# The mixer begins on half of K while the other half's modulation still loads

## The chip, the cores and the metric

One core of one Trainium2 chip runs the whole program. The metric is the device time of one execution in microseconds. Five engines work beside one another, each in the order of its own queue: TensorE (PE in the rows), VectorE (DVE), ScalarE (ACT), GpSimd (POOL) and SyncE (SP), which here only issues transfers. A transfer is issued by an engine's queue (SPq, ACTq) and carried out by 16 DMA engines.

## The reference

A first block (a mixer of forgetting attention and a gated linear recurrence, then a product-key expert layer, "peer"), and a second block (an S5 state-space layer, then an attention layer with compressed, selected and windowed keys), on 256 tokens of width 2048, all in float32. What matters for the change is the beginning of the first block:

```python
sc = jax.nn.silu(c)
mod = sc @ w_ada[l] + b_ada[l]                    # (1, 2048) @ (2048, 12288)
sh1, sc1, ga1, sh2, sc2, ga2 = jnp.split(mod, N_ADA, axis=-1)
h = _rmsnorm(x, g_mix[l]) * (1.0 + sc1[:, None, :]) + sh1[:, None, :]
...
proj = h @ w_in                                   # q, k, v, f, lx, ly
```

`sh1` and `sc1` must be known before `h`, and `h` before every projection. `w_ada` falls into twelve blocks of 1024 columns: 0 and 1 are `sh1`, 2 and 3 `sc1`, 4 and 5 `ga1`, 6 to 9 `sh2` and `sc2`, 10 and 11 `ga2`. Channels 0 to 1023 of `h`, the first half of K of the projections, need blocks 0 and 2 alone; channels 1024 to 2047 need 1 and 3. The second block has 16 such blocks more (`mod_w0`, `kv_mod_w`, `mod_w1`).

## The kernel before

Activations lie transposed, as sixteen tiles of 128 channels by 256 tokens. A product in near-float32 precision is made of three fp32r products: weights and activations are each split into a high and a low part. A half of a weight strip (128 x 1024, 0.52 MB, eight k) is loaded by SyncE into `raw` (four buffers), cast on ScalarE to `wh` and subtracted on VectorE or GpSimd to `wl` (three buffers each; `half`, L335). For each k, `step_b` (L353) multiplies `wh` with both parts of the activation, which lie side by side, in one product of 512 columns, and `wl` with the high part in one of 256; `ev` (L409) adds the two results. For the values, `lin_a` (L389) has the activations as the stationary side and makes three products of 512 columns.

The modulation is a product of one vector with a wide matrix (`gemv`, L284). In the form `big` it is summed on TensorE: chunks of 2 MB come into the four `xs` buffers, and four small products per k (`columns`, L291) add up in `pg`. Otherwise chunks of 0.52 MB come into `graw` (two buffers) from SyncE's queue (L299), and VectorE multiplies and adds them in `gacc` (L310, L312) if a buffer for it is open, with TensorE only for the sum over partitions. This form is a generator in `self.bg`: every weight strip's `tick` (L167) advances it by `self.rate` steps; at the end of a block it yields `PAUSE` up to three times, each of which ends the steps of that tick; `need` runs what is left, and `pace` (L185) sets a rate from it.

`start` (L515) loads blocks 0, 2, 1, 3 in the form `big` (16 loads of 2 MB), forms the two normed halves of `h` with `normed` (L468, its first operation is L473) and, between them, the set-up of the S5 layer (`s5_setup`, L1033): arithmetic on VectorE, then sixteen steps of `turn` (its first operation is L1126), drained before the mixer. `self.gate` puts the first weight loads behind the 13th of the 16 in SyncE's queue. Then come q (five strips at a time on their first halves), k, f, v, lx, ly and `w_out`; meanwhile the background runs at 1.5 steps a tick, at 3 during lx and ly, and through `w_out` at a rate that `pace` sets so that block 9 (`ffn`) is done. The order on each queue is laid down when the program is built, by priority in the order of the code and by when operands and buffers are free in a model of the run.

Of the kernel before, what the change touches and what calls it, by code (L numbers as in the profile page):

```python
# [9 lines left out]
F = mybir.dt.float32  # L10
# [3 lines left out]
AF = mybir.ActivationFunctionType  # L14
OP = mybir.AluOpType
# [15 lines left out]
TR = 0.45  # L31
TB = 1
NS1 = 5
NET = 4
MP = 1
# [7 lines left out]
NN = 3  # L43
NQ = 5
GA = 12
S2 = 2.5
# [31 lines left out]
COLS = {}  # L78
PAUSE = 2


# [75 lines left out]
class K:  # L157
    def __init__(self, tc, A, dbg=None):
        self.tc, self.nc, self.A = tc, tc.nc, A
        self.dbg = dbg or {}  # L160
        self.full = True
        self.nw, self.pool_share, self.srate = 0, 0, 1
        self.bg, self.side, self.par, self.loads = [], [], [], []
        self.loaded, self.gate, self.gp, self.hold, self.mid = None, None, None, None, False
        self.rate, self.owed, self.sowed, self.towed, self.slow = 1.5, 0.0, 0.0, 0.0, None

# [115 lines left out]


    def gemv(self, w, blocks, which, bias, out, big=False):  # L284
        nc = self.nc
        for b in blocks:
# [9 lines left out]
            for k in range(KD):  # L296
                if not big:
                    raw = self.sb.tile([128, 1024], F, name="graw", tag="graw", bufs=2)
                    nc.sync.dma_start(raw, w[128 * k:128 * k + 128, c0])  # L299
                else:  # L300
                    if k % 4 == 0:
                        rt = self.xs(F).rearrange("p a b t -> p (a b t)").rearrange("p (a c) -> p a c", a=4)
                        self.loads.append(
                            nc.sync.dma_start(rt, w[128 * k:128 * k + 512, c0].rearrange("(a p) c -> p a c", a=4)))
                    raw = rt[:, k % 4]
                ck = self.cact[:, 16 * which + k:16 * which + k + 1]
                if acc is None:
                    columns(ck.to_broadcast([128, 32]), raw, k == 0, k == KD - 1)
                elif k == 0:
                    nc.vector.tensor_scalar(acc, raw, ck, None, op0=OP.mult)  # L310
                else:
                    nc.vector.scalar_tensor_tensor(acc, raw, ck, acc, op0=OP.mult, op1=OP.add)  # L312
                if k < KD - 1:
                    yield True
# [199 lines left out]

    def start(self, x):  # L515
        nc, A, cp = self.nc, self.A, self.cp
        mod = self.mod = cp.tile([128, 96], F, name="mod")
        first = self.gemv(A["w_ada"], (0, 2, 1, 3), 0, self.col("b_ada", 0, 96), mod, big=True)
        for _ in range(8):
            next(first)  # L520
        with self.after(self.loads[0]):
            nc.sync.dma_start(x, A["xT"])
        next(first)
        acc = None
        for k in range(KD):
            acc = self.ssq(acc, x[:, k], k == KD - 1)
        r = self.rstd(acc, D)
        g = cp.tile([128, KD], F, name="gm", tag="gm", bufs=2)
        self.hs = []
        for h in range(2):  # L530
            blocks = 0
            while blocks < 2:
                blocks += not next(first)
                if h == 1 and blocks == TB:
                    next(turn, None)
            c = slice(8 * h, 8 * h + 8)
            nc.vector.scalar_tensor_tensor(g[:, c], mod[:, 16 + 8 * h:24 + 8 * h], 1.0, self.col("g_mix", 8 * h, 8),
                                           op0=OP.add, op1=OP.mult)
            self.hs.append(self.xs())
            self.normed([x[:, k] for k in range(KD)[c]], r, g[:, c], mod[:, c], [self.hs[h]])  # L540
            if h == 0:
                turn, store = self.s5_setup()
                self.side.append(store)
        self.drain([turn])
        self.gate = self.loads[GA]

    def mixer(self, x):
        with self.phase("ph_set") as self.ph:
            self.start(x)
        with self.phase("ph_mixer") as self.ph:  # L550
            self._mixer(x)

    def _mixer(self, x):
        nc, A, sb, cp = self.nc, self.A, self.sb, self.cp
        mod, hs = self.mod, self.hs
        bias = self.col("b_ada", 0, 96)
        self.use_pool(self.ph if GP[0] else None)
# [10 lines left out]
        qk = self.xs(F)  # L568
        for h, p in enumerate(self.lin_bs(A["w_q"], hs, NQ)):
            self.ev(p, qk[:, h, 0], 128 ** -0.5)  # L570
            self.gate = None
        for h in range(8):
            self.ev(self.lin_b(A["w_k"][h], hs), qk[:, h, 1])

        pf = self.lin_b(A["w_f"][0], hs)
        fl = self.s1()[:8]
        f2 = self.s1()[:8]
        nc.scalar.activation(f2, pf[:8, 0], AF.Identity, bias=self.col("b_f")[:8])
        nc.vector.tensor_add(fl, pf[:8, 1], f2)
        ft = self.ph.tile([128, 16], F, name="ft")  # L580
# [27 lines left out]
        self.par.append(decay())  # L608

        va = self.xs(F)  # L610
        vn = va.rearrange("p a b t -> p (a b t)")[:, :2048].rearrange("p (t c) -> p t c", t=2)
        at = va.rearrange("p a b t -> p (a b t)")[:, 2048:].rearrange("p (h t) -> p h t", h=8)
        for c in range(2):
            pp = self.lin_a(A["w_v"][c], hs)
            for t in range(2):
                nc.scalar.copy(vn[:, t, 512 * c:512 * c + 512], pp[t])
        lw = self.t8()
        lwf = lw.rearrange("p a b -> p (a b)")
        nc.sync.dma_start(lwf, A["lru_w"])
        aa, sq, ix = self.t8(), self.t8(), self.t8()  # L620
        ms = [self.xs(), self.xs()]
# [55 lines left out]
        for n in range(8):  # L677
            lx = self.ph.tile([128, T + 3], F, name="lx", tag="lx", bufs=2)
            nc.gpsimd.memset(lx[:, :3], 0.0)
            self.ev(self.lin_b(A["w_lx"][n], hs), lx[:, 3:])  # L680
            g = gates(n, lx)
# [350 lines left out]

    def s5_setup(self):  # L1033
        nc, A, sb, cp = self.nc, self.A, self.sb, self.cp
# [58 lines left out]
        def cmul(o, xr, xi, y):  # L1093

            wr, wi, yr, yi = wide(xr), wide(xi), y[:, :, 0], y[:, :, 1]
            t = self.sb.tile([128, 1024], F, name="graw", tag="graw", bufs=2)
            t = t.rearrange("p (k j c) -> p k j c", k=16, j=4)
# [7 lines left out]
            yield True  # L1105

        b, bb, c = big(), big(), big()
        flat = lambda m: m.rearrange("p k i j c -> p (k i j c)")
# [505 lines left out]
```

## Time and profile before

| | us |
|---|---|
| median of 3 runs | 3625.65 (3624.92 to 3626.92) |
| the profiled execution | 3617.7 |
| its span | 3616.0 |

| engine | busy us | share of the span |
|---|---|---|
| TensorE | 3294.4 | 91% |
| VectorE | 2652.5 | 73% |
| ScalarE | 1700.7 | 47% |
| GpSimd | 1066.7 | 29% |

The stages, as the trace places them: the start until 121 us, q, k, f and v until 292, lx and ly until about 440, `w_out` from 430 to 585, the router and the experts from 605 to 2390, S5 until about 2700, the second attention until the end. A table of busy time by stretch shows which engine is full in which stage; a wait names the engine that came last. Matmuls overlap their weight loads, and their ends are modelled, so the distance between two starts is read for the cost of one, not its duration.

### The profile page before, as it was taken

To read this page: it belongs to the slowest core of one execution; us is meant where nothing else is said; L and a number is where in the kernel's file an instruction comes from. 1 tells how busy PE (TensorE), PEld (TensorE's weight loads), DVE (VectorE), ACT (ScalarE), POOL (GpSimd) and SP (SyncE) were. 2 spreads that over 40 slices of the span, in tenths; PEclk is the share of its full clock that TensorE was granted. 3 is DMA by queue.
4 is the path that set the end of the run, shared out by engine and by line. 5 is a ranking of instruction groups with operands and counts; after the bars stand their busy time and mean duration, and the time that the engine had idled before them with its cause. 6 is when DMAs were issued, how large, how long until landed. Compare 5 with 4: busy or idle time off the path is not lost.

```text
span 3616.0 us, 50453 instructions
## 1 busy us (share of the span) xinstructions
PE 3294.4 (91%) x18446; PEld 2726.2 (75%) x18446; DVE 2652.5 (73%) x4072; ACT 1700.7 (47%) x2789; POOL 1066.7 (29%) x892
## 2 busy tenths in 40 slices
PE   4988778999999999999999989988989989999998
PEld 1676666878777777777777777767878878888886
DVE  4778987997657778887777767779886565666665
ACT  1534544455544444554444433354545544555553
POOL 1123345666522121211211233035452320122223
PEclk7999989999999999999999999989999999999999
DMA  9697676567779888888888878744435556444444
GB/s 398 235 301 252 203 234 228 163 223 262 243 250 314 300 281 291 293 285 279 293 286 278 293 268 269 267 158 139 147 127 186 186 167 198 160 155 149 159 143 144
DMA packets 260409, 832.47 MB, mean 230 GB/s; under 512 B 25792, under 2 KB 66880, under 8 KB 257472
## 3 DMA queue, kind: packets, MB, share of 16 engines
q1 hardware_dynamic: 258096, 829.11, 68.0%
q8 instruction: 145, 2.38, 0.3%
q14 instruction: 104, 0.85, 0.1%
q10 hardware_dynamic: 2064, 0.13, 0.0%
HBM read 797.56 MB, written 31.59 MB: 229 GB/s over the span
## 4 chain that ended last, share of the span: by engine, by line
PE 46%; DVE 14%; DMA 13%; issue 6%; POOL 3%; ACT 1%; SPq 0%; DVEq 0%; POOLq 0%; ACTq 0%
PE p L357 22%; PE p L358 11%; DVE wl L346 5%; DMA graw<-mod_w 5%; DMA graw<-kv_mod_w 3%; PE pm L929 2%; PE pm L928 2%; PE pm L930 2%; DVE gacc L312 2%; DMA s5d<-tb 2%; DMA raw<-peer_u 1%; DVE xs L1286 1%; PE pm L882 1%; ACT wh L342 1%; POOL xs L913 1%
## 5 line engine op out<-in xcount | busy, mean ns | idle before, releaser
L357 PE MATMUL p<-xs,wh 128*128 128x512 f32 x5600 | 2038.6, 406 | 43.5 <-DVE xs L476 19.9
L358 PE MATMUL p<-xs,wl 128*128 128x256 f32 x5600 | 1595.6, 285 | 47.6 <-DVE wl L346 40.4
L342 ACT CAST wh<-raw 128x1024 fp32r<-128x1024 f32 x996 | 1038.4, 1048 | 1124.6 <-PE p L357 408.9
L346 DVE TENSOR_TENSOR wl<-raw,wh 128x1024 fp32r<-128x1024 f32 x904 | 1151.4, 1281 | 511.0 <-ACT wh L342 501.4
L357 PEld LDWEIGHTS p<-xs,wh 128*128 128x128 f32 x5600 | 1069.5, 191 | 321.1 <-issue 39.0
L358 PEld LDWEIGHTS p<-xs,wl 128*128 128x128 f32 x5600 | 1078.4, 193 | 74.5 <-DVE wl L346 58.3
L312 DVE SCALAR_TENSOR_TENSOR gacc<-graw,cact,gacc 128x1024 f32<-128x1024 f32 x315 | 448.8, 1425 | 154.5 <-DMA graw<-mod_w 90.2
L929 PE MATMUL pm<-wl,xs 128*128 128x512 f32 x1024 | 411.7, 402 | 25.3 <-DVE wl L346 24.7
L928 PE MATMUL pm<-wh,xs 128*128 128x512 f32 x1024 | 409.4, 400 | 24.2 <-DVE vacc L937 18.8
L930 PE MATMUL pm<-wh,xs 128*128 128x512 f32 x1024 | 405.8, 396 | 0.0
L346 POOL TENSOR_TENSOR wl<-raw,wh 128x1024 fp32r<-128x1024 f32 x92 | 231.8, 2524 | 305.1 <-ACT wh L342 273.1
L909 POOL TENSOR_TENSOR t<-t,t 128x256 f32<-128x256 f32 x128 | 138.3, 1114 | 589.3 <-DMA t<-wd 589.3
L929 PEld LDWEIGHTS pm<-wl,xs 128*128 128x128 f32 x1024 | 196.2, 192 | 85.1 <-DVE wl L346 45.6
L913 POOL TENSOR_TENSOR xs<-t,xs 128x256 fp32r<-128x256 f32 x128 | 150.6, 1207 | 355.0 <-ACT xs L911 354.9
L928 PEld LDWEIGHTS pm<-wh,xs 128*128 128x128 f32 x1024 | 196.0, 191 | 74.9 <-DVE vacc L937 22.1
L930 PEld LDWEIGHTS pm<-wh,xs 128*128 128x128 f32 x1024 | 196.3, 192 | 39.7
L439 POOL TENSOR_TENSOR ssq<-ssq,s 128x256 f32<-128x256 f32 x96 | 105.4, 1107 | 237.7 <-ACT s L435 235.8
L898 ACT ACTIVATE t<-et 128x256 f32<-128x256 f32 x128 | 53.8, 420 | 209.4 <-DVE et L414 209.2
L413 ACT COPY et<-p 128x256 f32<-128x256 f32 x281 | 102.2, 364 | 31.2 <-PE p L358 31.1
L1528 POOL TENSOR_SCALAR t<-t,st 128x128 f32<-128x128 f32 (+1 forms) x64 | 77.6, 1224 | 128.0 <-DVE st L1526 128.0
L872 DVE TENSOR_SCALAR xs<-iof,eT,eT 128x128 f32<-128x128 f32 x192 | 82.2, 487 | 37.9 <-PE pm L882 37.9
L414 DVE TENSOR_TENSOR et<-p,et 128x256 f32<-128x256 f32 x224 | 93.1, 416 | 10.3 <-ACT et L413 10.3
(392 smaller groups left out, 3126.3 us busy)
## 6 DMA issues: line engine op xcount, KB each, us to landing
raw<-peer_u SPq DMA_DIRECT2D x256, 512.0 KB, 5.3
raw<-peer_v SPq DMA_DIRECT2D x256, 512.0 KB, 5.6
graw<-mod_w SPq DMA_DIRECT2D x192, 512.0 KB, 5.6
graw<-w_ada SPq DMA_DIRECT2D x128, 512.0 KB, 4.8
raw<-nsa_z SPq DMA_DIRECT2D x96, 512.0 KB, 3.7
xs<-w_ada SPq DMA_DIRECT2D x16, 2048.0 KB, 13.1
graw<-kv_mod_w SPq DMA_DIRECT2D x64, 512.0 KB, 5.7
raw<-w_out SPq DMA_DIRECT2D x32, 512.0 KB, 5.1
```

Of the source, the lines that this page charges most:

```text
L312: nc.vector.scalar_tensor_tensor(acc, raw, ck, acc, op0=OP.mult, op1=OP.add)
L342: nc.scalar.copy(h, s)
L346: (nc.gpsimd if on_pool else nc.vector).tensor_sub(l, s, h.bitcast(F))
L357: self.nc.tensor.matmul(p, h[:, sl], x, start=k == 0, stop=False, skip_group_check=True)
L358: self.nc.tensor.matmul(p[:, 1], l[:, sl], x[:, 0], start=False, stop=k == KD - 1, skip_group_check=True)
L413: nc.scalar.copy(t, p[:, 0])
L439: nc.gpsimd.tensor_add(acc[0], acc[0], sq)
L909: nc.gpsimd.tensor_mul(gc, gc, wv[:, c])
L913: nc.gpsimd.tensor_sub(ap[:, c - 2, 1], gs[:, c - 2], ap[:, c - 2, 0].bitcast(F))
L928: nc.tensor.matmul(pp[t], ah, h[:, sl], start=c == 0, stop=False, skip_group_check=True)
L929: nc.tensor.matmul(pp[t], ah, l[:, sl], start=False, stop=False, skip_group_check=True)
L930: nc.tensor.matmul(pp[t], ap[:, c, 1, 128 * t:128 * t + 128], h[:, sl], start=False, stop=c == 7, skip_group_check=True)
```

## The change

`start` loads only blocks 0 and 2 in the form `big` (8 loads of 2 MB). The square sums and the whole S5 arithmetic are traced before the modulation's end, two turns go beside each of the last four steps, and the remaining eight become a generator that each tick advances by one. Weight loads are put behind the 6th of the 8 loads (`GA` 5).

Then the mixer runs in two passes. The first works on the first half of K alone: the eight halves of `w_q`, of `w_k`, the one of `w_f`, both column halves of `w_v`, and four strips of `w_lx` (`NL`). It uses `sum_b`, which makes three products of 256 columns per k into one result, and stores the partial sums (`qk`, `f2`, `vn`, `ix`). Meanwhile blocks 1 and 3 are a background entry `mix`, at 1.85 steps a tick (`RA`); as no `gacc` is open then, its chunks are summed by TensorE. The other blocks wait (`hold` is `ga1`). When `mix` is done the second normed half is made. The second pass does the second halves of the same strips and adds the partial sums; there the background goes on at 0.75 steps a tick (`R1 / 2`), with a tick for every half strip of q, k and f and every strip of v. The rest of lx, ly and `w_out` are as before.

All small modulation chunks, those of the later stages too, are issued from ScalarE's queue by `fetch_chunk`, up to two ahead (`DEEP`), into three `graw` buffers instead of two. The ring `et` has three buffers instead of four. Cut to its core:

```diff
-NET = 4
+NET = 3
-NQ = 5
-GA = 12
+GA = 5
+NL = 4
+RA = 1.85
+DEEP = 2
+    def fetch_chunk(self):
+        if self.chunks:
+            src = self.chunks.pop(0)
+            raw = self.sb.tile([128, 1024], F, name="graw", tag="graw", bufs=3)
+            self.nc.scalar.dma_start(raw, src)
+            self.ahead.append(raw)
...
                 if not big:
-                    raw = self.sb.tile([128, 1024], F, name="graw", tag="graw", bufs=2)
-                    nc.sync.dma_start(raw, w[128 * k:128 * k + 128, c0])
+                    while not self.ahead:
+                        self.fetch_chunk()
+                    raw = self.ahead.pop(0)
...
+                if not big:
+                    while len(self.ahead) < DEEP and self.chunks:
+                        self.fetch_chunk()
...
-        first = self.gemv(A["w_ada"], (0, 2, 1, 3), 0, self.col("b_ada", 0, 96), mod, big=True)
+        first = self.gemv(A["w_ada"], (0, 2), 0, self.col("b_ada", 0, 96), mod, big=True)
...
+        turn, store = self.s5_setup(norm)
+        for n, _ in enumerate(first):
+            if n >= 20:
+                next(turn)
+                next(turn)
+        self.side += [turn, store]
+        self.gate = self.loads[GA]
...
+    def sum_b(self, src, i):
+        self.tick()
+        h, l = self.half(src, i)
+        self.gate = None
+        p = self.p2()[:, 0]
+        for k in range(8):
+            x = self.hs[i][:, k]
+            sl = slice(128 * k, 128 * k + 128)
+            self.nc.tensor.matmul(p, h[:, sl], x[:, 0], start=k == 0, stop=False, skip_group_check=True)
+            self.nc.tensor.matmul(p, h[:, sl], x[:, 1], start=False, stop=False, skip_group_check=True)
+            self.nc.tensor.matmul(p, l[:, sl], x[:, 0], start=False, stop=k == 7, skip_group_check=True)
+        return p
...
-        for n, b in (("ga1", (4, 5)), ("ffn", range(6, 10)), ("ga2", (10, 11))):
+        for n, b in (("mix", (1, 3)), ("ga1", (4, 5)), ("ffn", range(6, 10)), ("ga2", (10, 11))):
...
-        self.rate, self.hold = R1, "ga2"
+        self.rate, self.hold = RA, "ga1"
+        self.pool_share = MP2
+        self.first_half(x, r, 0)
...
+        for h in range(8):
+            nc.scalar.activation(qk[:, h, 0], self.sum_b(A["w_q"][h], 0), AF.Copy, scale=128 ** -0.5)
+        for h in range(8):
+            nc.scalar.copy(qk[:, h, 1], self.sum_b(A["w_k"][h], 0))
+        nc.scalar.activation(f2, self.sum_b(A["w_f"][0], 0)[:8], AF.Identity, bias=self.col("b_f")[:8])
+        values(0)
+        for n in range(NL):
+            nc.scalar.copy(ix[:, n], self.sum_b(A["w_lx"][n], 0))
+            late()
+        self.need("mix")
+        late()
+        self.use_pool(self.ph if GP[0] else None)
+        self.rate, self.hold = R1 / 2, "ga2"
         self.pool_share = MP
...
-            self.ev(self.lin_b(A["w_k"][h], hs), qk[:, h, 1])
+            nc.vector.tensor_add(qk[:, h, 1], self.sum_b(A["w_k"][h], 1), qk[:, h, 1])
```

`values(i)` is `lin_a` for one half of K, `late` makes the second normed half as soon as `mix` is done, and `first_half` holds the lines that formed one normed half in `start`.

## Rows read from the trace of the kernel before

**Rows 1.** The page: span, then busy time, share and instructions of an engine.
```profile
span 3616.0 us, 50453 instructions
...
PE 3294.4 (91%) x18446; PEld 2726.2 (75%) x18446; DVE 2652.5 (73%) x4072; ACT 1700.7 (47%) x2789; POOL 1066.7 (29%) x892
```

**Rows 2.** Busy time by stage: us, engines (instructions), PEclk, DMA share, GB/s.
```profile
core 0: us, PE busy (x) PEld busy (x) DVE busy (x) ACT busy (x) POOL busy (x), PEclk, DMA share, GB/s
0.00:57.00 57.00, 24.21 (x264) 10.56 (x264) 9.63 (x32) 9.56 (x23) 11.04 (x21) 0.84 0.99 396
57.00:121.00 64.00, 44.02 (x387) 24.85 (x387) 48.03 (x168) 30.40 (x92) 0.00 (x0) 0.77 0.76 294
121.00:290.00 169.00, 149.87 (x753) 122.77 (x753) 130.05 (x172) 65.66 (x84) 30.94 (x15) 0.96 0.87 287
290.00:430.00 140.00, 112.49 (x612) 95.39 (x612) 129.02 (x199) 75.38 (x165) 56.44 (x36) 0.94 0.67 219
430.00:505.00 75.00, 47.67 (x229) 39.31 (x228) 64.83 (x105) 26.24 (x49) 18.71 (x10) 0.77 0.65 211
505.00:605.00 100.00, 85.08 (x479) 67.54 (x478) 76.17 (x94) 44.10 (x71) 57.51 (x38) 0.95 0.75 256
```

**Rows 3.** Timeline of the start: start us, us, engine, line, operation, tiles, count.
```profile
54.42 1.28 DVE L473 SCALAR_TENSOR_TENSOR s<-x,gm,rstd 128x256 f32<-128x256 f32 x3
...
83.41 0.69 ACT L1126 ACTIVATE pad<-t,rmask 128x128 f32<-128x128 f32 x2 [12.00 <-DVE t L1104]
...
120.79 0.50 PE L357 MATMUL p<-xs,wh 128*128 128x512 f32 x1
```

**Rows 4.** Timeline of TensorE: products of w_q, and the last two of w_v.
```profile
123.45 0.40 PE L357 MATMUL p<-xs,wh 128*128 128x512 f32 x1
...
123.68 0.28 PE L358 MATMUL p<-xs,wl 128*128 128x256 f32 x1
...
123.80 0.40 PE L357 MATMUL p<-xs,wh 128*128 128x512 f32 x1
...
291.65 0.39 PE L403 MATMUL pm<-wl,xs 128*128 128x512 f32 x1
291.88 0.39 PE L405 MATMUL pm<-wh,xs 128*128 128x512 f32 x1
```

**Rows 5.** Modulation loads issued from 95 to 292, and from 292 to 605.
```profile
graw<-w_ada SPq DMA_DIRECT2D x36, 512.0 KB, 5.5
...
graw<-w_ada SPq DMA_DIRECT2D x67, 512.0 KB, 4.4
```

**Rows 6.** Timeline: twelve of the modulation's small products on TensorE.
```profile
102.60 1.06 PE L293 MATMUL pg<-xs,cact 128*32 128x256 f32 x12
```

**Rows 7.** The page's groups: busy, mean ns of one, then idle before.
```profile
L312 DVE SCALAR_TENSOR_TENSOR gacc<-graw,cact,gacc 128x1024 f32<-128x1024 f32 x315 | 448.8, 1425 | 154.5 <-DMA graw<-mod_w 90.2
```

**Rows 8.** Timeline of VectorE at the end of w_out: the modulation's last steps.
```profile
571.82 1.75 DVE L312 SCALAR_TENSOR_TENSOR gacc<-graw,cact,gacc 128x1024 f32<-128x1024 f32 x1
585.67 0.17 DVE L331 TENSOR_TENSOR mod<-pm,cols 128x8 f32<-128x8 f32 x1 [3.63 <-PE pm L329]
```

**Rows 9.** Waits from 120 to 560: us in total, times, longest.
```profile
DVE gacc L312 <- DMA graw<-w_ada: 21.7, 16, 2.8
```

**Rows 10.** Waits from 1030 to 2200, beside the experts.
```profile
ACT wh L342 <- PE pm L930: 227.5, 114, 9.3
DVE wl L346 <- ACT wh L342: 121.1, 93, 6.7
DVE gacc L312 <- DMA graw<-mod_w: 71.5, 54, 3.8
DVE gacc L312 <- DMA graw<-kv_mod_w: 40.2, 37, 2.8
PE p L358 <- DVE wl L346: 25.2, 25, 2.9
PE pm L929 <- DVE wl L346: 22.6, 31, 2.0
```

**Rows 11.** SyncE's waits from 1030 to 2200, and ScalarE's one load (timeline).
```profile
SPq L339 <- DVE wl L346: 447.4, 233, 7.5
SPq L299 <- DVE gacc L312: 109.7, 83, 3.7
...
120.44 0.39 ACTq L1147 DMA_DIRECT2D s5d<-direct  x1
```

More of the change, by code (lines that the diff above doesn't have):

```diff
@@ L281, in consts, with _gemv @@
         nc.vector.tensor_scalar(self.cact, self.cact, 0.5, None, op0=OP.mult)
-    def gemv(self, w, blocks, which, bias, out, big=False):
+    def fetch_chunk(self):
[4 more added lines that the diff above has]
+            self.ahead.append(raw)
+    def gemv(self, w, blocks, which, bias, out, big=False):
+        nc = self.nc
+        if not big:
+            self.chunks += [w[128 * k:128 * k + 128, 1024 * b:1024 * b + 1024] for b in blocks for k in range(KD)]
+        return self._gemv(w, blocks, which, bias, out, big)
+    def _gemv(self, w, blocks, which, bias, out, big):
         nc = self.nc
@@ L522, in start @@
             nc.sync.dma_start(x, A["xT"])
[L523 to L528, printed above, removed]
-        self.hs = []
[L530 to L543, printed above, removed]
@@ L544, in start, with norm @@
-        self.drain([turn])
-        self.gate = self.loads[GA]
+        rs = []
+        def norm():
+            acc = None
+            for k in range(KD):
+                acc = self.ssq(acc, x[:, k], k == KD - 1)
+            rs.append(self.rstd(acc, D))
+        turn, store = self.s5_setup(norm)
[5 more added lines that the diff above has]
+        self.gate = self.loads[GA]
+        self.g0 = cp.tile([128, KD], F, name="gm", tag="gm", bufs=2)
@@ new lines, in start, with first_half @@
+        self.hs = []
+        return rs[0]
+    def first_half(self, x, r, h):
+        c = slice(8 * h, 8 * h + 8)
+        g, mod = self.g0, self.mod
+        self.nc.vector.scalar_tensor_tensor(g[:, c], mod[:, 16 + 8 * h:24 + 8 * h], 1.0,
+                                            self.col("g_mix", 8 * h, 8), op0=OP.add, op1=OP.mult)
+        self.hs.append(self.xs())
+        self.normed([x[:, k] for k in range(KD)[c]], r, g[:, c], mod[:, c], [self.hs[h]])
+    def sum_b(self, src, i):
[10 more added lines that the diff above has]
+        return p
@@ new lines, in _mixer, with late, values @@
+        fl = self.ph.tile([8, T], F, name="fl")
+        ix = self.t8()
+        def late():
+            if len(hs) == 1 and self.bg[0][0] != "mix":
+                self.first_half(x, r, 1)
+        def values(i):
+            for c in range(2):
+                pp = [self.pm(), self.pm()]
+                for a in range(2):
+                    w = self.wload(A["w_v"][c][2 * i + a])
+                    for kk in range(4):
+                        k = 4 * a + kk
+                        h, l = w[kk // 2]
+                        sl = slice(512 * (kk % 2), 512 * (kk % 2) + 512)
+                        for t in range(2):
+                            xh, xl = (hs[i][:, k, j, 128 * t:128 * t + 128] for j in range(2))
+                            nc.tensor.matmul(pp[t], xh, h[:, sl], start=k == 0, stop=False, skip_group_check=True)
+                            nc.tensor.matmul(pp[t], xh, l[:, sl], start=False, stop=False, skip_group_check=True)
+                            nc.tensor.matmul(pp[t], xl, h[:, sl], start=False, stop=k == 7, skip_group_check=True)
+                    if i == 0:
+                        late()
+                        self.tick()
+                for t in range(2):
+                    o = vn[:, t, 512 * c:512 * c + 512]
+                    if i == 0:
+                        nc.scalar.copy(o, pp[t])
+                    else:
+                        nc.vector.tensor_add(o, o, pp[t])
@@ L579, in _mixer @@
-        nc.vector.tensor_add(fl, pf[:8, 1], f2)
+            nc.vector.scalar_tensor_tensor(qk[:, h, 0], self.sum_b(A["w_q"][h], 1), 128 ** -0.5, qk[:, h, 0],
+                                           op0=OP.mult, op1=OP.add)
+        for h in range(8):
+            nc.vector.tensor_add(qk[:, h, 1], self.sum_b(A["w_k"][h], 1), qk[:, h, 1])
+        nc.vector.tensor_add(fl, self.sum_b(A["w_f"][0], 1)[:8], f2)
         ft = self.ph.tile([128, 16], F, name="ft")
@@ L608, in _mixer @@
         self.par.append(decay())
[L610 to L616, printed above, removed]
+        values(1)
         lw = self.t8()
@@ L679, in _mixer @@
             nc.gpsimd.memset(lx[:, :3], 0.0)
[L680 removed]
+            if n < NL:
+                nc.vector.tensor_add(lx[:, 3:], self.sum_b(A["w_lx"][n], 1), ix[:, n])
+            else:
+                self.ev(self.lin_b(A["w_lx"][n], hs), lx[:, 3:])
             g = gates(n, lx)
@@ L1105, in cmul @@
             yield True
+        before()
         b, bb, c = big(), big(), big()
```

27 lines of the change are left out of this document (12 added, 15 removed).

## The prediction

> **What bounds the kernel now.** I read the page first, then the busy time stage by stage, then the order of work around the first product, then the waits. The profiled execution took 3617.7 us, of which the span is 3616.0 [rows 1]; the median of the runs, 3625.65, is 8 us above it. I sum against 3617.7 and add the 8 us at the end. 0.2% of the time, about what a measurement of this kernel can tell from no change, is 7 us.
>
> TensorE carries the kernel in most places, but not at the start and not evenly. The busy time by stage [rows 2] is read by column. Until 57 us DMA is full (0.99 of its engines) and TensorE runs only the modulation's vector products. From 57 to 121 us DMA falls to 0.76 and TensorE still has no projection: the first normed half begins at 54.4, yet the first w_q product stands at 120.8 [rows 3], since blocks 1 and 3 of w_ada (another 16.8 MB) are loaded ahead of any weight, and then come the sixteen padded turns of the S5 set-up, from 83.4. From 121 to 290 TensorE (150 of 169 us) and DMA (0.87) are both near full. From 290 to 505 it is VectorE: 194 of 215 us busy. In w_out, 505 to 605, TensorE has 85 and VectorE 76 of 100. So an earlier start gains time only if the later stages don't fill with what it pushed back.
>
> **What the change does, part by part.**
>
> *Start.* The first stage now loads 8 chunks of 2 MB, not 16, so the normed first half comes where it comes now, at 54.4. The S5 arithmetic, most of VectorE's 48 us from 57 to 121, and eight turns go under these loads, where VectorE has 9.6 us of work in 57 [rows 2]. Four weight chunks and up to three modulation chunks of 0.52 MB now come in the same time: 3.7 MB at 396 GB/s [rows 2] is 9 us if all are ahead of the last block. I take 60 us for the first product, with 55 and 79 as ends; 79 is eight turns on the path at (120.8 - 83.4)/16 = 2.3 us [rows 3].
>
> *Up to the last value product.* Before, that is at 292 [rows 4]. The new order has 54 halves of weights up to there: 17 (q, k, f) + 8 (v) + 4 (lx) in the first pass, 17 + 8 in the second. In [rows 4] a 512-column product is followed after 0.23 us and a 256-column one after 0.12, with another weight load each time. So a half of the new form, 24 products of 256 columns, costs 2.9 us against 8 x 0.35 = 2.8 now; a half of values is 12 x 0.23 = 2.7. 38 x 2.9 + 16 x 2.7 = 153 us. The 32 chunks of modulation are 128 small products of 1.06/12 = 0.09 us [rows 6]: 11 us. The eight turns left take some 10 us of TensorE. Together 174; at the share that TensorE reaches from 121 to 290 (0.89) it is 196, and the end 256. DMA says about the same: 28.3 MB of weights (54 x 0.52), 24 MB of modulation (46 x 0.52) and 4.2 MB of S5 stores (four of 1 MB) at 287 GB/s [rows 2] are 197 us from 57, end 254. I take 254, a gain of 38 us. At a full TensorE it would be 58; with the late start, 17 to 19.
>
> *What is pushed back.* The background sums of the other modulation blocks stand still in the first pass and run at 0.75 of a step per tick in the second: some 14 chunks up to 292, where 36 have gone now [rows 5]. The 22 others must be summed before the router needs them. The stages of w_lx and w_ly keep their rate of 3 and are VectorE's already, so they can't take more. They land in w_out, whose rate is set from what is left. 22 x 1.43 us [rows 7] is 31 us of VectorE and 11.5 MB. VectorE's idle time from 290 to 605 is 315 - 270 = 45 us [rows 2], so the cost lies between 0 (all hidden) and 31/0.86 = 36 (VectorE no fuller than it is). It is nearer to the upper end: now the last block's sum just fits under w_out (last step at 571.8, its values out at 585.7 [rows 8]), each end of a block makes the pace pause for three ticks, and whatever is left is run with nothing beside it. I take 24.
>
> *w_lx.* Four halves fewer here, each with a subtraction on VectorE or GpSimd, and sums that stall less: VectorE waited 21.7 us for modulation chunks between 120 and 560 [rows 9]. Between 0 and 20; I take 8.
>
> *The loads of the modulation beside the experts, 1030 to 2200.* The sixteen blocks of mod_w and kv_mod_w are 256 chunks. In [rows 10] VectorE waits 71.5 + 40.2 us for them, and TensorE waits 25.2 + 22.6 = 48 us for VectorE's low halves, which are queued behind those sums. In SyncE's queue a modulation chunk stands behind weight loads that wait for a free buffer: 447 us in 233 waits, and the modulation issues themselves 110 us in 83 [rows 11]. With three buffers, two loads ahead and another queue, most of the 112 us should go. The gain is between 0 and 48; not every one of TensorE's waits comes from there (VectorE also waits 121 us for ScalarE's casts), so I take half, 24.
>
> *ScalarE.* Each load is now an instruction of ScalarE: 0.39 us for the one it has [rows 11]. Behind it queue the casts, behind these VectorE's subtractions and TensorE. After the first pass there are 24 blocks of 16 such loads; 384 x 0.39 us are 150 us on an engine busy 47% [rows 1]. Casts are late for VectorE for 121 of 1170 us [rows 10], a tenth, while ScalarE itself waits far more often for TensorE. A tenth of 150 is 15; the other end is 0, and I take 8. The `et` ring goes from four buffers to three: only w_ly's gelu holds three at once, 8 tiles, 0 to 8 x 1.43 = 11 us with the sum's length as the nearest row; I take 2, as VectorE is the late engine there and ScalarE would wait for it anyway.
>
> *Sum.* -38 + 24 - 8 - 24 + 8 + 2 = -36: 3617.7 - 36 = 3581.7, and with the 8 us 3590.
>
> **The rivals.**
>
> 1. *Another queue brings nothing.* From 121 on, DMA's engines are 0.87 busy [rows 2]; if VectorE's waits are for bytes and not for the place in the queue, loading two ahead moves them without removing them, and the 24 us stay: 3614. For it: after 57 us no stretch of [rows 2] goes above 0.87. Against: SyncE's own waits for buffers [rows 11]. [...]
>
> 2. *ScalarE becomes the late engine (slower).* Its queue is in order: where a load waits for its buffer, which VectorE's sum must free, the casts behind it wait too. SyncE's wait for that was 109.7/83 = 1.3 us at a time [rows 11]. From 0.11 us per chunk that reaches TensorE, (36 + 8)/384, the gain is gone. If half the 384 chunks put their 0.39 us on the path, 75 us replace the 8: 3657. For it: VectorE's 121 us of waiting for casts. Against: ScalarE's casts wait 227.5 us for TensorE to free a buffer [rows 10], so they mostly run ahead. [...]
>
> 3. *The early start is handed back.* The turns keep the first product at 79, and the pushed-back sums cost the full 36: -17 + 36 - 8 - 24 + 8 + 2 = -3: 3623. This is also the case in which the change doesn't do what it says. For it: the stages from 290 to 505 are VectorE's and take no more.
>
> 4. *All goes well.* 58 at the start, 8 handed back, 12 and 40 from the waits, 2 for ScalarE: -100, 3526.
>
> **How the numbers follow.** The forecast has 0.45, rival 1 0.17, rival 2 0.13, rival 3 0.10, rival 4 0.15. Faster by over 0.2%: 0.45 + 0.17 + 0.15 = 0.77; within: 0.10; slower: 0.13. The range leaves out rival 2 and the lower half of rival 4: 3528 to 3632.
>
> **What would show it.** In the changed profile: the first w_q product at 55 to 65 (79 or later: rival 3); the last value product near 254; the modulation chunks in ScalarE's queue; more of them after 430, and the end of w_out with a stretch of sums that nothing covers; VectorE's wait for modulation chunks down from 112 us in the expert stage, and TensorE's wait for low halves with it (down alone: rival 1); casts that VectorE waits for well above 121 us would be rival 2. The prediction is wrong if the time from the router on is longer than now, or if what is gained by 292 is not there at 605.

## The result: the changed kernel is slower

| | us |
|---|---|
| median after (4 runs) | 3651.66 (3647.10 to 3656.81) |
| median before, beside it | 3625.28 |
| ratio | 1.0075, 95% interval 1.0055 to 1.0095 |
| the profiled execution after, its span | 3656.8, 3654.7 |

The forecast was 3590 with a range from 3528 to 3632: the sign is wrong, and the time lies outside the range. Rival 2, ScalarE as the late engine, at 3657, is the case that came. The two profiled runs lie 39 us apart, the medians 26; what follows is read from the profiled runs.

The page of the changed kernel has the same busy times as [rows 1], within 2% but for GpSimd; the 39 us that the span is longer are time in which engines wait.

```profile
span 3654.7 us, 51412 instructions
...
PE 3292.4 (90%) x18782; PEld 2753.8 (75%) x18782; DVE 2643.3 (72%) x4069; ACT 1696.9 (46%) x2787; POOL 1105.9 (30%) x899
```

The busy time by stage of the changed kernel, columns and stretches as in [rows 2]:

```profile
0.00:57.00 57.00, 18.59 (x174) 10.54 (x177) 37.89 (x127) 15.41 (x41) 14.84 (x24) 0.73 0.99 396
57.00:121.00 64.00, 54.70 (x506) 41.24 (x498) 23.81 (x77) 32.01 (x86) 7.07 (x3) 0.95 0.60 198
121.00:290.00 169.00, 147.07 (x1046) 126.99 (x1046) 88.74 (x94) 59.58 (x76) 48.27 (x18) 0.95 0.86 290
290.00:430.00 140.00, 102.57 (x546) 86.78 (x546) 113.41 (x234) 63.91 (x144) 37.87 (x30) 0.88 0.46 154
430.00:505.00 75.00, 49.30 (x232) 40.25 (x230) 61.45 (x89) 27.23 (x49) 23.59 (x12) 0.81 0.69 235
505.00:605.00 100.00, 64.70 (x335) 53.73 (x336) 67.33 (x75) 31.58 (x51) 32.14 (x25) 0.80 0.70 230
```

VectorE's arithmetic did move under the first loads (37.9 us in the first 57, 9.6 before), but from 290 to 430 DMA stands at 0.46 where it was 0.67, and over the stretch no engine is full: TensorE 102.6 of 140, VectorE 113.4. That points to waits, not to one full engine.

Where the time went is read from the weight loads. The view of the line that issues them (L359; L339 before) gives, for each weight, the number of issues and the first and the last start. In the changed kernel:

```profile
L359 SPq DMA_DIRECT2D raw<-peer_v x256: 327/328/1476, 1157.8 to 2403.7; - x128
...
L359 SPq DMA_DIRECT2D raw<-w_out x32: 327/328/328, 460.4 to 613.5; - x32
L359 SPq DMA_DIRECT2D raw<-peer_w_q x32: 327/328/328, 618.4 to 749.0; - x32
...
L359 SPq DMA_DIRECT2D raw<-w_ly x16: 327/328/373, 362.1 to 452.9; - x16
```

The same view of every kernel gives this table (us in the span; the difference to before in brackets). Its kernels are named in the experiments. One program profiled twice (tp_sp and tp_sp_ga7, below) differs by 3 to 9 us in these columns, so smaller differences say nothing.

| | w_ly, last | w_out, last | peer_w_q, last | peer_v, first | peer_v, last | ratio to before |
|---|---|---|---|---|---|---|
| before | 429.0 | 566.8 | 680.2 | 1089.4 | 2364.8 | |
| after | 452.9 (+24) | 613.5 (+47) | 749.0 (+69) | 1157.8 (+68) | 2403.7 (+39) | 1.0075 |
| tp_sp | 405.7 (-23) | 566.1 (-1) | 683.0 (+3) | 1092.9 (+4) | 2344.7 (-20) | 0.9946 |
| tp_old | 405.9 (-23) | 565.3 (-2) | 718.0 (+38) | 1117.9 (+29) | 2373.2 (+8) | 1.0042 |
| p_act | 448.6 (+20) | 590.1 (+23) | 708.7 (+29) | 1131.5 (+42) | 2382.8 (+18) | 1.0040 |
| p_sp | 428.6 (0) | 571.6 (+5) | 689.5 (+9) | 1094.0 (+5) | 2344.6 (-20) | 0.9947 |
| tp_late_act | 408.0 (-21) | 567.9 (+1) | 684.6 (+4) | 1095.3 (+6) | 2333.2 (-32) | 0.9914 |

So the changed kernel is ahead at the first w_q product (75.1 against 120.8), 24 us behind by the end of w_ly, 68 behind at the experts, and gets 30 back beside them.

*The start.* TensorE's timeline has the new products, and VectorE's the first operation of the normed half, which was at 54.42 [rows 3]:

```profile
73.05 2.06 DVE L493 SCALAR_TENSOR_TENSOR s<-x,gm,rstd 128x256 f32<-128x256 f32 x5
...
75.78 0.28 PE L582 MATMUL p<-xs,wl 128*128 128x256 f32 x1
75.90 0.27 PE L580 MATMUL p<-xs,wh 128*128 128x256 f32 x1
```

Two products of 256 columns start 0.12 us apart, as taken from [rows 4]. The half itself comes 19 us later than before.

*The clearest stall* is in the second pass. ScalarE's and TensorE's timelines, in the changed kernel:

```profile
288.10 0.39 PE L632 MATMUL pm<-wh,xs 128*128 128x512 f32 x1
305.99 0.59 PE L680 MATMUL pm<-ident,ft 128*8 128x128 f32 x2 [17.50 <-DVE ft L676]
...
288.57 1.04 ACT L362 CAST wh<-raw 128x1024 fp32r<-128x1024 f32 x1 [1.66 <-PE pm L632]
...
293.76 19.54 ACTq L291 DMA_DIRECT2D graw<-w_ada  x9
313.40 1.05 ACT L362 CAST wh<-raw 128x1024 fp32r<-128x1024 f32 x1 [19.46 <-DMA graw<-w_ada]
```

Nine modulation loads stand in ScalarE's queue one behind the other, 19.54 / 9 = 2.2 us a load, though the issue takes 0.33. Each waits for its buffer, which a sum on VectorE must free; a sum takes 1.28, and steps of the forget gate and 4.4 us of waits for chunks to land stand between the sums. The next cast of a weight stands behind the loads for 19.5 us.

TensorE's stop of 17.5 us has another releaser: it waits for the forget gate (`ft`), whose steps on VectorE alternate with the sums. VectorE is busy for 15.0 us of that time, and TensorE restarts at a granted clock of 0.50, its products of 512 columns 0.43 us apart until about 309 and 0.23 from there:

```profile
288.50:306.00 17.50, 0.01 (x1) 0.01 (x2) 15.02 (x38) 1.25 (x2) 1.01 (x1) 0.61 0.77 262
306.00:309.40 3.40, 3.40 (x10) 2.63 (x11) 3.34 (x7) 0.00 (x0) 0.00 (x0) 0.50 0.73 240
```

Between the gate's first step on VectorE and its last (L673, L676) stand ten sums here; in tp_sp, the same program with SyncE's queue, there stands one, and the wait for `ft` is 2.4 us (before: 1.8). So another queue for the loads has also changed the order in which VectorE's work was laid down.

*The tail of w_out.* In the busy time by stretch of the changed kernel TensorE is busy for 11.7 and then 6.7 of 20 us:

```profile
620.00:640.00 20.00, 11.68 (x53) 9.43 (x52) 11.59 (x11) 3.19 (x5) 7.90 (x5) 0.83 0.68 233
640.00:660.00 20.00, 6.70 (x50) 2.83 (x49) 13.31 (x17) 4.20 (x6) 6.40 (x3) 0.69 0.84 278
```

The last sums of the modulation for the router run here with little beside them, as forecast; in [rows 8] they ended under w_out.

### The profile page after: what moved, and what is told of

Read it like the earlier page. It is cut to its first block, busy times and chain, and to the rows that moved or that the text cites. A ratio compares the mean times of both kernels' runs of the same rounds, so it can differ in the third digit from the quotient of the medians.

```text
span 3654.7 us, 51412 instructions
## 1 busy us (share of the span) xinstructions
PE 3292.4 (90%) x18782; PEld 2753.8 (75%) x18782; DVE 2643.3 (72%) x4069; ACT 1696.9 (46%) x2787; POOL 1105.9 (30%) x899
## 4 chain that ended last, share of the span: by engine, by line
PE 55%; DVE 19%; DMA 13%; issue 6%; POOL 2%; ACT 2%; DVEq 0%; ACTq 0%; POOLq 0%; SPq 0%
PE p L377 24%; PE p L378 12%; DVE wl L366 6%; DMA graw<-mod_w 5%; DMA graw<-w_ada 3%; PE pm L1009 3%; PE pm L1010 3%; PE pm L1008 3%; DVE gacc L329 3%; DMA s5d<-tb 2%; DMA graw<-kv_mod_w 1%; PE pm L962 1%; DVE xs L1367 1%; ACT wh L362 1%; DMA raw<-peer_v 1%
## 5 line engine op out<-in xcount | busy, mean ns | idle before, releaser
L377 PE MATMUL p<-xs,wh 128*128 128x512 f32 x5296 | 1938.7, 408 | 66.5 <-DVE xs L496 32.3
L378 PE MATMUL p<-xs,wl 128*128 128x256 f32 x5296 | 1513.3, 286 | 74.7 <-DVE wl L366 71.0
L377 PEld LDWEIGHTS p<-xs,wh 128*128 128x128 f32 x5296 | 1017.2, 192 | 330.3 <-issue 37.3
L378 PEld LDWEIGHTS p<-xs,wl 128*128 128x128 f32 x5296 | 1024.0, 193 | 100.7 <-DVE wl L366 87.9
L329 DVE SCALAR_TENSOR_TENSOR gacc<-graw,cact,gacc 128x1024 f32<-128x1024 f32 x315 | 429.9, 1365 | 130.0 <-DMA graw<-mod_w 56.3
L1009 PE MATMUL pm<-wl,xs 128*128 128x512 f32 x1024 | 403.9, 394 | 25.5 <-DVE wl L366 25.5
L1008 PE MATMUL pm<-wh,xs 128*128 128x512 f32 x1024 | 402.8, 393 | 1.8 <-DVE vacc L1017 1.8
L1010 PE MATMUL pm<-wh,xs 128*128 128x512 f32 x1024 | 400.7, 391 | 0.0
L993 POOL TENSOR_TENSOR xs<-t,xs 128x256 fp32r<-128x256 f32 x128 | 158.3, 1267 | 788.5 <-ACT xs L991 788.2
L366 POOL TENSOR_TENSOR wl<-raw,wh 128x1024 fp32r<-128x1024 f32 x99 | 256.2, 2593 | 361.7 <-ACT wh L362 347.3
L989 POOL TENSOR_TENSOR t<-t,t 128x256 f32<-128x256 f32 x128 | 151.5, 1219 | 138.1 <-DMA t<-wd 87.6
L582 PE MATMUL p<-xs,wl 128*128 128x256 f32 x336 | 100.8, 301 | 10.8 <-DVE wl L366 6.4
```

Source lines behind the costliest of these rows:

```text
L366: (nc.gpsimd if on_pool else nc.vector).tensor_sub(l, s, h.bitcast(F))
L377: self.nc.tensor.matmul(p, h[:, sl], x, start=k == 0, stop=False, skip_group_check=True)
L378: self.nc.tensor.matmul(p[:, 1], l[:, sl], x[:, 0], start=False, stop=k == KD - 1, skip_group_check=True)
L582: self.nc.tensor.matmul(p, l[:, sl], x[:, 0], start=False, stop=k == 7, skip_group_check=True)
L989: nc.gpsimd.tensor_mul(gc, gc, wv[:, c])
L993: nc.gpsimd.tensor_sub(ap[:, c - 2, 1], gs[:, c - 2], ap[:, c - 2, 0].bitcast(F))
```

## The experiments

The theory after the result (W): ScalarE's in-order queue is the cause, since loads that wait for a buffer hold the casts and casts that wait for TensorE hold the loads. The rivals: the two passes themselves, or the deeper loading whatever queue it uses. (The letters of the theories in the expectations are chosen anew for each group of runs.) All kernels keep the arithmetic of the reference unless their expectation says otherwise.

**One part at a time.** p_act is the kernel before with the new loading alone (three buffers, two ahead, ScalarE's queue, `NET` 3); p_sp is the same from SyncE's queue; tp_sp is the changed kernel with SyncE's queue; tp_old has the two passes with the old loading.

```diff
 # p_sp against p_act, and tp_sp against the changed kernel
-            self.nc.scalar.dma_start(raw, src)
+            self.nc.sync.dma_start(raw, src)
 # tp_old against the changed kernel: issued when used, bufs=2, NET = 4
-                    while not self.ahead:
-                        self.fetch_chunk()
-                    raw = self.ahead.pop(0)
+                    raw = self.sb.tile([128, 1024], F, name="graw", tag="graw", bufs=2)
+                    nc.sync.dma_start(raw, w[128 * k:128 * k + 128, c0])
```

> The kernel before with the new loading of the modulation alone: three buffers, two chunks ahead, from ScalarE's queue, et in three buffers; no two passes. Theory A (the two passes lose the time and the loading gains it beside the experts): 25 to 40 us faster than before, some 3590 to 3600, with the gain between the first peer_v load and the last, as in the changed kernel (69 us late at the one, 39 late at the other). Theory B (loads in ScalarE's queue hold up its casts everywhere): as slow as the changed kernel or nearly, 3640 or more.

> The same, but the chunks are issued from SyncE's queue, as before: three buffers and two chunks ahead alone. Theory A with the queue as its cause: within 10 us of before, since the chunks still stand behind weight loads that wait. Theory A with the depth as its cause: 20 to 40 us faster, as p_act. Theory B: clearly faster than p_act.

> The changed kernel with its chunks issued from SyncE's queue, still two ahead in three buffers. Theory B (in the two passes a cast stands behind a load that waits for its buffer, as from 294 to 313 us): the last value product comes before 295 instead of at 320, and the kernel takes 3620 or less. Theory A: the two passes are late by themselves; the last value product stays at 310 or later, and the kernel takes 3650 or more.

> The two passes alone: chunks from SyncE's queue when they are used, two buffers, et in four. Theory A: slower than the changed kernel by what the loading gains beside the experts, some 30 us: 3675 to 3690, and 60 to 70 us late at the router already. Theory B: not slower than the changed kernel, and at the router less than 40 us late.

Measured: p_act 3636.96, ratio 1.0040 (1.0024 to 1.0056); p_sp 3598.04, 0.9947 (0.9927 to 0.9967); tp_sp 3598.08, 0.9946 (0.9932 to 0.9960); tp_old 3634.53, 1.0042 (1.0021 to 1.0063). That is theory B: tp_sp has its last value product at 283.0 and stays under 3620, tp_old is 38 us late at the router, and p_act lies just under the 3640 that B asked for. One word in one line is worth 39 us in one pass by the medians (3636.96 - 3598.04; 34 by the ratios) and, by the ratios, 1.3%, 47 us, in two. From SyncE's queue the whole change is 0.5% faster than the kernel before. The two passes add nothing to the loading (tp_sp as p_sp): they lead by 23 us at w_ly and by 5 at the end of w_out. tp_old loses 39 us between w_out and the router's last load; what of the old loading costs that there is not settled.

The waits from 120 to 610 show who waits longer. p_act:

```profile
DVE wl L366 <- ACT wh L362: 42.0, 25, 5.1
DVE gacc L329 <- DMA graw<-w_ada: 40.0, 31, 6.1
...
PE p L378 <- DVE wl L366: 27.6, 12, 9.0
...
ACT wh L362 <- DVE gacc L329: 11.2, 2, 8.2
```

p_sp, the same stretch:

```profile
DVE wl L366 <- ACT wh L362: 30.6, 32, 4.2
...
DVE gacc L329 <- DMA graw<-w_ada: 11.9, 10, 3.0
...
PE p L378 <- DVE wl L366: 7.8, 6, 2.4
```

From ScalarE's queue VectorE waits 40 us for chunks instead of 12, for casts 42 instead of 31, and TensorE waits 28 us for low halves instead of 8. ScalarE's casts wait 11.2 us for sums that free a load's buffer, 3.5 in p_sp. The transfers are no slower: the median from issue to landing of a modulation chunk is 5.4 us in p_act and 5.2 in p_sp, of a w_out half 5.0 in both. One thing these runs cannot separate: with the other queue VectorE's and TensorE's orders change as well, from about 90 us on, and no run changes the queue and keeps the orders. So the 39 us belong to the change of queue; how much of them is the loads' own waiting and how much the new orders is not shown.

**The place in the queue.** p_act_late puts each load behind the next cast of a weight half.

```diff
-        nc.scalar.copy(h, s)
+        cast = nc.scalar.copy(h, s)
+        while len(self.ahead) < DEEP and self.chunks:
+            with self.after(cast):
+                self.fetch_chunk()
```

> The kernel before with three buffers, two chunks ahead and ScalarE's queue, as p_act, but each load is put in the queue behind the cast of the next weight half, by when the sum that frees its buffer lies a tick back. Theory W (the queue costs by waiting: casts stand behind a load whose buffer is not free): the 38 us that p_act lost to p_sp up to the first peer_v load come back for the most part, some 3605 or less. Theory I (it costs by the issue itself, 0.33 us of ScalarE for each of 384): stays near p_act's 3637.

Measured: 3642.29, ratio 1.0059 (1.0037 to 1.0082), no better than p_act. VectorE's wait for chunks from 120 to 610 rises from 40.0 to 49.7 us, and its wait for casts falls from 42.0 to 31.0. So with the casts ahead of the loads the chunks come later, and theory W in the form "only the wait for the buffer" fell; what stays is that either order holds somebody.

**The issue alone.** act_issue is p_sp with one more load of a single column per chunk, issued by ScalarE behind the last cast and read by nobody.

```diff
+            small = self.sb.tile([128, 1], F, name="small", tag="small", bufs=8)
+            with self.after(self.cast):
+                self.nc.scalar.dma_start(small, self.A["cols"][:, :1])
```

> p_sp, and with each chunk ScalarE issues one more load of a single column into a small ring of its own, behind the last cast and with no buffer to wait for: the issue alone, without its wait. It adds 384 loads that nothing reads. Theory W: within 8 us of p_sp, some 3598 to 3606. Theory I: 25 us or more slower than p_sp.

Measured: 3617.70, ratio 0.9981 (0.9967 to 0.9996). Against p_sp that is 12 us by the ratios and 20 by the medians of the two sets of runs: more than theory W allowed and less than theory I asked, between a third and a half of p_act's loss by the same measure. The run is not the issue alone, as the 384 extra loads of 0.5 KB are also moved. I put the rest down to the coupling through buffers and to the changed orders; that is inferred.

**Where it costs.** tp_late_act is tp_sp with ScalarE's queue only from the S5 tables on, beside the second half of the experts; p_late_act the same in one pass; p_act_front the reverse of that, ScalarE's queue only up to there.

```diff
+        self.on_act = True         # at the S5 tables; p_act_front: from True to False
-            self.nc.sync.dma_start(raw, src)
+            (self.nc.scalar if self.on_act else self.nc.sync).dma_start(raw, src)
```

> The changed kernel, with SyncE issuing the chunks up to the tables of the S5 layer and ScalarE those beside the second half of the experts. If the queue costs only where VectorE is late with the sums (both passes, w_lx to the router), this takes tp_sp's time, some 3598, within 8 us. If it costs something beside the experts too, it is 10 us or more slower than tp_sp.

> p_sp (one pass, three buffers, two ahead) with ScalarE issuing the chunks only from the S5 tables on, beside the second half of the experts: tp_late_act without the two passes. Theory Q (the two passes bring nothing in the end, the loading alone does): 3583 to 3597, within 6 us of tp_late_act, 3589.0. Rival (two passes bring part of their 23 us): 3605 or more, that is, slower than tp_late_act by over 12 us.

> p_act with SyncE issuing the chunks from the S5 tables on; ScalarE issues them in the mixer, the router and the first half of the experts. Theory F (the whole cost lies in front of that point): as p_act, ratio 1.000 to 1.006, first peer_v load at 1125 to 1136 (p_act 1131.5, p_sp 1094.0). Rival E (half or more lies beside the second half of the experts): ratio 0.990 to 0.998.

Measured: tp_late_act 3589.0, ratio 0.9914 (0.9886 to 0.9941), the fastest kernel that keeps all the arithmetic; p_late_act 3613.66, 0.9977 (0.9962 to 0.9992); p_act_front 3625.30, 1.0015 (0.9995 to 1.0036), with the first peer_v load at 1125.3. That ScalarE's queue costs ahead of the S5 tables is shown: p_act_front is 31 us behind p_sp at the first peer_v load (1125.3 against 1094.0), and p_act and p_sp need the same time from the first to the last peer_v load (1251.3 and 1250.6). By the times it is the larger part, not the whole: p_act_front loses 25 of p_act's 34 us by the ratios. The table says where: against p_sp, p_act is 20 us late at the end of w_ly, still 19 at the router's last load, and 38 at the first peer_v load, so one half arises in w_lx and w_ly and the other in the router's arithmetic and the first half of the experts. Beside the experts' second half its sign differs: 0.3% faster in two passes, 0.3% slower in one, each just outside the intervals. By its time p_late_act falls to the rival, that the two passes bring part of their gain; but of the 25 us between it and tp_late_act only 11 are there at the first peer_v load (1106.0 and 1095.3), and the rest arises beside the experts, where both run the same code. A repeat alone can differ by 9 us at that load. What the two passes are worth with the better queue isn't settled.

**Another queue.** p_pool is p_sp with the chunks from GpSimd's queue.

```diff
-            self.nc.sync.dma_start(raw, src)
+            self.nc.gpsimd.dma_start(raw, src)
```

> p_sp (one pass, three buffers, two ahead) with the modulation chunks issued from GpSimd's queue instead of SyncE's (p_sp 3598.0, ratio 0.9947) or ScalarE's (p_act 3637.0, 1.0040). Theory C (the cost is that of ScalarE's own stream: the casts of the weights and the evictions stand behind the loads and the loads behind them): GpSimd has few instructions in the mixer, so the kernel stays near p_sp, 3590 to 3610, and the last w_ly load near 428.6, not 448.6. Rival M (any second queue costs it, because two queues load side by side and the weights get fewer bytes): near p_act, 3628 to 3646, last w_ly load 440 or later.

Measured: 3716.75, ratio 1.0266 (1.0225 to 1.0306), far above both expectations: my theory C, that only ScalarE's stream of casts makes the cost, is wrong. The last w_ly load at 445.3 is as rival M has it, but its reason isn't seen: of the mixer's weights from 120 to 610 only w_v lands later after its issue (6.1 us in p_pool, 5.1 in p_sp, in the median), and w_out lands after 4.7 us where p_sp has 5.0. The larger loss comes later: from the first to the last peer_v load p_pool needs 1327.7 us, p_sp 1250.6. The waits of p_pool from 1090 to 2330:

```profile
POOL graw L291 <- DVE gacc L329: 310.7, 128, 6.4
...
POOL graw L291 <- DVE gacc L327: 259.8, 8, 44.9
...
DVE gacc L329 <- DMA graw<-mod_w: 90.4, 44, 8.5
PEld p L378 <- DVE wl L366: 89.3, 49, 9.9
POOL xs L933 <- ACT xs L931: 83.3, 10, 34.0
```

GpSimd stands for up to 44.9 us in front of a load whose buffer VectorE hasn't freed, and its own work for the experts (`xs`, `t`) shares that queue. The issues alone keep GpSimd busy for 209 us (384 of 0.54), which no run separates from the waits. So both engines tried that have work of their own lose by it; SyncE has none, and a load that waits there, as for 1.9 us at a time in the kernel before (447.4 us in 233 waits [rows 11]), holds only other transfers.

**The sums that are pushed back.** tp_sp_r1 has the background at `R1` in the second pass instead of `R1 / 2`. tp_sp_less and p_sp_less leave out 22 chunks of the router's modulation.

```diff
-        self.rate, self.hold = R1 / 2, "ga2"        # tp_sp_r1
+        self.rate, self.hold = R1, "ga2"
+    def nk(self, w, b):                             # tp_sp_less, p_sp_less
+        return 5 if w is self.A["w_ada"] and b in (8, 9) else KD
```

> tp_sp with the background at 1.5 steps a tick in the second pass instead of 0.75. Theory P (tp_sp's 23 us at the last w_ly load are lost in w_out and the router to the sums pushed back): w_ly's last load some 15 us later than in tp_sp, but the lead kept to the router, and up to 15 us faster than tp_sp. Rival: those sums cost the same wherever they are put: within 5 us of tp_sp.

> tp_sp (two passes, chunks from SyncE's queue) with 22 chunks fewer of the modulation: blocks 8 and 9 of w_ada (sc2 of the router) are summed over 5 of their 16 chunks, so that these two blocks are not the reference's; the pace through w_out is set for what is left. 22 is the number of sums that the two passes push back behind the last value product. Theory P (the 23 us that the two passes have gained by the last w_ly load, 405.7 against 428.6 in p_sp, are handed back in w_out because these sums of 1.43 us find no room on VectorE): the last w_out load comes at 535 to 548 instead of 566, and the median is 3560 to 3580 instead of 3598. Rival D (handed back for another reason: the order of casts and buffers, or the products themselves): last w_out load within 8 us of 566, median above 3590.

> The same 22 chunks left out (blocks 8 and 9 of w_ada summed over 5 of 16 chunks, so these two blocks are not the reference's) in p_sp, the order of before with one pass. Theory P: in one pass most of these sums lie beside work that leaves room, so leaving them out gains less than in tp_sp: last w_out load 560 to 568 instead of 571.6, median 3588 to 3596. Rival D: it gains as much as in tp_sp, since the sums cost the same in either order; then the two passes' gain is not lost to them.

Measured: tp_sp_r1 3600.34, ratio 0.9936 (0.9916 to 0.9956), as tp_sp, which is the rival's case: at w_ly it has lost the lead (430.5 against 405.7), and the end of w_out comes 8 us later (574.3). tp_sp_less 3575.85, 0.9872 (0.9848 to 0.9896), last w_out load 543.5; p_sp_less 3588.75, 0.9898 (0.9871 to 0.9924), last w_out load 557.3. The first is as theory P has it; the second gains less than the first, as P has it too, but more than P's 560 to 568 allows. Without 22 sums the end of w_out comes 22.6 us earlier in two passes and 14.3 in one: 1.03 and 0.65 us a sum. So the sums, with their loads, cost about three quarters of their duration (1.4 us) in two passes and under half of it in one. The two passes' lead at the end of w_out grows from 5.5 to 13.8 us, so the sums explain about half of the 17 us that are handed back; the other half isn't explained. A count in the traces also corrects the 22: up to the last value product VectorE has made 34 sums in the kernel before and 21 in tp_sp, so 13 are pushed back behind it, and 16 behind the last w_ly load (62 against 46).

**The first half earlier.** tp_sp_ga7 puts the weights behind all eight 2 MB loads (`GA` 7).

> tp_sp with GA 7 instead of 5: the first weight halves are put behind the last of the eight 2 MB loads instead of behind the sixth. In the kernel after, the first normed half came at 73.0 (54.4 before) and the first w_q product at 75.1. Theory L (the weights and chunks that load early take bytes from the last two 2 MB blocks): the normed half comes at 54 to 60, the first product within 6 us behind it, and the last value load is 5 to 15 us earlier. Rival S (the S5 arithmetic and the turns, now traced ahead, hold VectorE and TensorE): normed half stays at 68 or later; then the weights come later too, and the kernel is 3 to 8 us slower than tp_sp.

Measured: 3600.43, ratio 0.9930 (0.9904 to 0.9956). The edit did nothing: every engine's queue has the same order as in tp_sp, as SyncE's weight loads there already stood behind the eighth. So the expectation isn't tested, and the run is a repeat of tp_sp: 0.9946 and 0.9930, with the first peer_v load at 1092.9 and 1101.6.

## Why the prediction was wrong

*ScalarE, +8: the step that failed.* I priced a load on ScalarE by its issue (0.39 us; it is 0.33) and by the share of casts that are late beside the experts, and took a tenth. Measured it is 34 to 39 us in one pass and 47 in two, four to six times as much. The share came from the wrong stage: beside the experts' second half ScalarE waits for TensorE (227.5 us in [rows 10]) and the loads cost little; most of the loss arises ahead of it, in w_lx and w_ly and from the router to the first half of the experts. And the tenth counted only the issue, and took VectorE's order as given. A load waits in the queue for its buffer, and rival 2 named this; its place, too, I left to the experts, and the sign I gave for it, casts late for VectorE well above 121 us there, did not come (126.8, below). That rival 2's 3657 is near the measured 3651.66 is in part luck: its 75 us are 28 too many, and the 44 us that its other terms still gain are 22 too many (with SyncE's queue the change brings 22). What rival 2 needs, that a cast waits behind the loads ahead of it in ScalarE's queue, is in the stall at 293.76: a cast stands for 19.5 us behind nine loads.

*Start, -38 at the last value product: mis-sized.* First product 75.1, not 60; last value product 319.9, not 254. Of the 66 us, 37 come with ScalarE's queue: in tp_sp the last is at 283.0. The other 29 were mine: 13 at the start (first product at 73.4 in tp_sp) and 16 in the passes, whose cause stays open. At the start I moved the S5 arithmetic ahead without its loads. SyncE's timeline of the kernel before has them here, behind the eighth block:

```profile
38.58 0.97 SPq L1111 DMA_DIRECT2D t<-s_bc  x2
```

In the changed kernel, with the end of the modulation on VectorE:

```profile
2.79 0.97 SPq L1192 DMA_DIRECT2D t<-s_bc  x2
...
69.58 0.17 DVE L351 TENSOR_TENSOR mod<-pm,cols 128x8 f32<-128x8 f32 x1 [3.63 <-PE pm L349]
```

Two loads of 1 MB now stand ahead of most of the blocks, by estimate 5 us at the 396 GB/s of [rows 2], beside the 3.7 MB of chunks and weights for which I had up to 9 and took less than 6. Together they are near the 16 us by which the modulation's values come later (69.58; before, 54.02). And from 69.58 to 73.05 VectorE has turns and a subtraction in its queue ahead of the normed half.

*w_lx, -8: not separated.* It is part of the two above; by w_ly the two passes with SyncE's queue are worth -23 where I had -46.

*Pushed back, +24: right in size in tp_sp*, where -23 at w_ly becomes -1 at the end of w_out, and the tail of w_out is as I described it. But only 13 sums were pushed back, not 22, and the sums explain about half of what is handed back, so the size is in part luck.

*Loads beside the experts, -24: right in size, wrong in cause.* The changed kernel regains 68.4 - 38.9 = 29.5 us between the first and the last peer_v load. But tp_old, with the old loading, regains 20 there. In a stretch as long as that of [rows 10], 1100 to 2270, the changed kernel has:

```profile
DVE wl L366 <- ACT wh L362: 126.8, 106, 2.9
DVE gacc L329 <- DMA graw<-mod_w: 53.8, 33, 4.8
...
PE p L378 <- DVE wl L366: 35.3, 27, 4.6
...
ACT wh L362 <- DVE gacc L329: 31.9, 14, 3.6
...
PE pm L1009 <- DVE wl L366: 25.0, 19, 3.4
DVE gacc L329 <- DMA graw<-kv_mod_w: 20.3, 16, 4.8
DVE gacc L327 <- DMA graw<-mod_w: 13.9, 1, 13.9
```

VectorE's wait for chunks fell only from 112 to 88 us, and TensorE's wait for low halves rose from 48 to 60. The steps I gave (chunks earlier, so low halves earlier, so TensorE earlier) did not happen. From the first to the last peer_v load the kernel before needs 1275 us, p_sp, p_act and tp_old 1251 to 1255: most of the gain may belong to an unlucky order in the kernel before, which several changes of the program undo. That is inferred, not shown by a run of its own.

*et, +2: not separated.* `NET` 3 is in p_sp, which is faster than before.

*Rival 1* (another queue brings nothing) has its reason borne out and its price not: p_act and p_sp need the same time from the first to the last peer_v load (1251.3 and 1250.6 us), and the changed kernel regains the 24 us and more, for another reason. *Rival 3* is close to what tp_sp shows up to the experts.

## What to carry to other kernels

A load issued from ScalarE or GpSimd, which compute, was here an instruction in that engine's order: nine of them waited for their buffers and a cast waited 19.5 us behind them on ScalarE, and GpSimd stood for up to 44.9 us in front of one. Price it by that wait, which goes by the pace of the engine that frees the buffers (2.2 us a load here, though the issue takes 0.33), in the stage where the engine's results are due next, and leave issuing to an engine that has nothing else to do unless a run says otherwise, as tp_late_act's does. Where a program's orders are laid down when it is built, look also at what the new queue did to the order on the other engines: ten sums came to stand ahead of a step that TensorE waited for. When work is moved ahead, move its loads with it in the sum, and read from the trace what then stands before them on the queue.

## What the runs showed that I had not expected

Identical bytes in identical tiles cost -22 us from SyncE's queue (p_sp), +17 from ScalarE's (p_act) and +92 from GpSimd's (p_pool), each by the medians against the kernel before; the page of p_pool has its loads as work of GpSimd, 0.54 us each:

```profile
L291 POOL DMA_DIRECT2D graw<-mod_w x192 | 104.0, 542 | 653.9 <-DVE gacc L327 255.2
```

Landing times hardly differ between the three (medians of 5.2 to 5.8 us from 120 to 610). And tp_sp and tp_sp_ga7, which turned out to be one program, differ by 2.5 us at w_ly, 7 at the router and 9 at the first peer_v load in their profiled runs: that much of a milestone is the run, not the kernel.
